# Two of layer two's three value chunks made with seven block products, beside the first eight key tiles

## The chip, the cores and the metric

The kernel runs on one core of a Trainium2 chip. The metric is device time in microseconds for one execution, from the start of the program to its end.

The engines are named as in the profile: PE is TensorE (matrix products into PSUM banks), PEld its weight loads, DVE is VectorE, ACT is ScalarE, POOL is GpSimd, and SP is the queue that starts most loads from HBM. "q" behind an engine's name means its sequencer. L629 is line 629 of the kernel before.

## The reference, cut to what matters

A two-layer decoder trunk on 256 positions of width 2048, in float32. Layer two's mixer takes one shared K and V from the normed residual stream, 12 heads of 128, and its queries from another norm of the same stream:

```
kv = _rmsnorm(x, g_kv) @ w_kv            # 2048 x 3072: K 1536 wide, V 1536 wide
k_sh, v_sh = split(kv, 2)
proj = _rmsnorm(x, nrm[0]) @ w_in_b      # q 1536 wide, qm 512 wide
o_sb = _stick_breaking(q, k_sh, v_sh)    # 12 heads, 256 queries, 256 keys
o_mem = _memory_attention(qm, mem, ...)  # 4 heads into 256 memory rows
heads = concat(o_sb, o_mem)
x = x + _rmsnorm(heads @ w_o); then the conv-gated MLP
```

V is thus 256 x 2048 times 2048 x 1536; the kernel makes it in three chunks of 512 columns.

## The kernel before, in words

**Products.** Every float32 operand is split into a rounded high part (fp32r, an ACT cast, L622) and the rest (a DVE subtraction, L623). A product takes three matmuls: high by high, low by high, high by low (`mm3`, L127). A projection whose output is wanted with positions along the free axis is made tile by tile, 128 features by 256 positions: `ws_tile` (L133) loads 1 MB of weights into one of three `raw` tiles, splits it in two halves into `whi` and `wlo` (four tiles each), and issues 16 pairs of a 512-column matmul (both parts of the input at once) and a 256-column one. `ws_pair` makes two such tiles into one `qk` tile (five of them) and multiplies by the row factors. A projection with positions along the partitions is made by chunks of 512 columns, `as_chunk` (L213): four pieces of 1 MB, 96 matmuls of 512 columns. `v_proj` (L515) is such a chunk, scaled by the row factors on the way out of PSUM.

**Seven products.** `wide` (L634) makes two chunks at once. The 256 positions are two blocks of 128, the two chunks are two blocks of columns, each pair of k tiles (a unit, eight in all) two blocks of depth; the 2 by 2 by 2 block product is done with seven products where eight is the plain count, 21 matmuls of 512 columns for a unit. It needs sums of blocks on both sides. Those of the input come from `sums_of_h` (L588): `make(i)` does five DVE operations, and a second step splits the result into `s`, here one tile of 32 KB a partition under the tag `h1`. Those of the weights are made as they come: `first_sums` (L626) loads 512 KB into a tile `d` by SP (L629) and adds another 512 KB to it by an accumulating transfer from POOL's queue (L630); `sums` (L664) takes `d` and the 768 KB of `raw` (L661) and makes a second tile `e` on DVE; `split_sums` (L680) splits `d` and `e` into the four `forms` under the tag `x`. Both `d` and `e` come from the tag `sh`, which has eleven tiles of 4 KB a partition (`bufs=11`, L66). Beside each unit runs one `ws_tile` in pieces, `ws_beside` (L152).

In `wide` nearly every instruction is pinned: it keeps the order of the program on its engine. In unit u the order is

```
PE    half of ws(u), products 1 2 3, other half of ws(u), products 7 5 6 4
SP    d(u+2), raw(u+1), weights of ws(u+1)
DVE   split d(u), split e(u), sums(u+1), split raw(u+1), add of ws(u), split weights of ws(u+1), also[u]
```

`then` is the next phase's weights, `also` a list of further steps by unit. Where an instruction is not pinned, a scheduler that plays the program through orders each engine's queue by what is ready, and a tile is handed out again when its last reader is done. `later(n, fn)` puts `fn` ahead of the n-th next piece or tile.

**Where it is used before.** In layer one for two value chunks beside eight q and k tiles (L1097), and in each MLP in five phases.

**Layer two's mixer before** (L1143 to L1163): the row factors; value chunk 0; `x_T` (L273), which transposes x on PE and writes its scaled high and low parts into `hq` (L269 on ACT, L270 on DVE); value chunks 1 and 2; four tiles of memory queries, `qm_proj`; then six times a pair of k tiles, a pair of q tiles, and `sb_pair` (L454), which puts the scores two tiles later, the transposes of the weights five and the output six tiles later. `mem_heads` (L323) puts the memory attention's steps beside the first of these tiles. At that point `sh` holds the memory keys `mk`, the memory values `mv`, the value chunks and `qm`.

Of the kernel before, what the change touches and what calls it, by code (L numbers as in the profile page):

```python
# [10 lines left out]
F32 = mybir.dt.float32  # L11
F32R = mybir.dt.float32r
BF16 = mybir.dt.bfloat16
AF = mybir.ActivationFunctionType
ALU = mybir.AluOpType
AX = mybir.AxisListType

P = 128
D = 2048
S = 256  # L20
# [4 lines left out]
KT = D // P  # L25
# [20 lines left out]
class Body:  # L46
# [538 lines left out]
        else:  # L585
            self.add_normed(ys, r[1], 1, each)

    def sums_of_h(self, h):  # L588

        nc, pin = self.nc, self.pin
        s = self.sb.tile([P, KT // 2, 4, 2, P], F32R, name="h1", tag="h1", bufs=1)

        def less(out, x, y):

            pin(nc.vector.scalar_tensor_tensor(out, x, -1.0, y, op0=ALU.mult, op1=ALU.subtract))

        def make(i):  # L600
            a, d = self.pairtile(), self.pairtile().rearrange("p a (b t) -> p (a b) t", b=2)
            hh = h[2][:, 2 * i:2 * i + 2, :, :].bitcast(F32)
            pin(nc.vector.tensor_add(a, hh[:, :, 0, :], hh[:, :, 1, :]))
            a1, a2 = a[:, :, 0:P], a[:, :, P:S]
            pin(nc.vector.tensor_sub(d[:, 0, :], a2[:, 1, :], a2[:, 0, :]))
            less(d[:, 1, :], d[:, 0, :], a1[:, 0, :])
            pin(nc.vector.tensor_sub(d[:, 2, :], a1[:, 0, :], a2[:, 0, :]))
            less(d[:, 3, :], d[:, 1, :], a1[:, 1, :])
            return lambda: self.split_heads(d, s[:, i, :, 0, :], s[:, i, :, 1, :])

        return s, make

# [21 lines left out]
    def wide(self, src, then, ahead, h, s, forms, r, beside, also, outs=None):  # L634

        nc, n = self.nc, KT // 2
        ps = {i: self.bank("g" if i in (1, 2, 6, 7) else "s") for i in range(1, 8)}
        pin, add = self.pin, nc.vector.tensor_add
        half = lambda f, i: f[..., i * 512:(i + 1) * 512]

        def lhs(i, u):
            if i in (1, 2, 4):  # L650
                kt, t = 2 * u + (i != 1), int(i == 4)
                return [h[2][:, kt, a, t * P:(t + 1) * P] for a in range(2)]
            return [s[:, u, {5: 0, 6: 1, 7: 2, 3: 3}[i], a, :] for a in range(2)]

        def product(i, u, f, at):
            self.mm3(ps[i], *lhs(i, u), half(f[0], at), half(f[1], at), u == 0, u == n - 1)

        def load(u):

            raw = self.sb.tile([P, 2048], F32, name="raw", tag="raw", bufs=3)  # L660
            pin(nc.sync.dma_start(raw[:, :1536], src[u][:, :1536]))  # L661
            return raw

        def sums(d, raw):  # L664

            e = self.sh([P, 1024])
            pin(add(half(e, 1), half(d, 0), half(raw, 2)))
            pin(add(half(e, 0), half(e, 1), half(raw, 0)))  # L668
            return d, e

        def plain(raw):
            fa, fb = ([self.sb.tile([P, 1024], F32R, name=k, tag=k, bufs=4) for k in ("whi", "wlo")]
                      for _ in range(2))
            self.split(*fa, raw[:, 0:1024])
            self.split(*(half(f, 0) for f in fb), half(raw, 2))
            return fa, fb

        summed = [[forms[:, 2 * i + j, :] for j in range(2)] for i in range(2)]

        def split_sums(t):  # L680
            for of, parts in zip(t, summed):
                self.split(*parts, of)

        raw = load(0)

        high, low = self.splits[-4]
        with self.tc.issue_after(high.ins), self.tc.issue_after(low.ins):
            t = sums(ahead.pop(0), raw)
            split_sums(t)
        b = beside[0]()  # L690
        next(b)
        next(b)
        f = plain(raw)
        self.pinned = True
        for u in range(n):
            more = u + 1 < n
            next(b)
            if u:
                split_sums(t)
            self.catch_up()  # L700
            fa, fb = f
            product(1, u, fa, 1)
            product(2, u, fa, 0)
            product(3, u, fb, 0)
            if u + 2 < n:
                ahead.append(self.first_sums(src, u + 2))
            elif then is not None:
                ahead.append(self.first_sums(then, u + 2 - n))
            if more:
                raw = load(u + 1)  # L710
                after = beside[u + 1]()
                t, f = sums(ahead.pop(0), raw), plain(raw)
            self.catch_up()
            next(b)
            next(b, None)
            if more:
                next(after)
                next(after)
            if u in also:
                also[u]()  # L720
            product(7, u, summed[0], 1)
            product(5, u, summed[0], 0)
            product(6, u, summed[1], 1)
            product(4, u, summed[1], 0)
            b = after
        g0, a, v0, v1 = outs() if outs else (self.sc([P, 512]) for _ in range(4))
        more = lambda out, x, i: pin(add(out, ps[i], x))

        def scaled(out, i, t):
            pin(nc.vector.scalar_tensor_tensor(out, ps[i], r[:, t:t + 1], out, op0=ALU.mult, op1=ALU.add))  # L730

        pin(nc.scalar.copy(a, ps[1]))
        pin(nc.scalar.activation(g0, ps[1], AF.Copy, scale=r[:, 0:1]))
        scaled(g0, 2, 0)
        more(a, a, 6)
        more(v0, a, 5)
        more(v0, v0, 3)
        more(a, a, 7)
        more(v1, a, 5)
        pin(nc.scalar.activation(a, a, AF.Copy, scale=r[:, 1:2]))  # L740
        scaled(a, 4, 1)
        self.pinned = False
        self.catch_up(-1)
        return (g0, a), (v0, v1)

    def ffn(self, layer, h, each, filler=None, done=None, late=None):
        nc = self.nc
# [240 lines left out]
    def run(self):  # L988
# [86 lines left out]
        qm = self.qm_proj(a["wqm_a"], h, 1)  # L1075

        forms = self.sb.tile([P, 4, 1024], F32R, name="x", tag="x", bufs=1)
        tiles, pairs, V = {}, {}, []

        def pair(j, out):  # L1080
            who = QK_ORDER[2 * j:2 * j + 2]
# [4 lines left out]
        def tile(u):  # L1086
            j, i = u // 2, u % 2
            if i == 0:
                pairs[j] = self.pairtile()
            done = lambda: self.behind_this(*pair(j, pairs[j]))  # L1090
            return self.ws_beside(pairs[j][:, i, :], a["wqk_a"][u], h, done if i else None)

        def outs():
            V.extend(self.sh([P, 2, 512]) for _ in range(2))
            return [v[:, t, :] for v in V for t in range(2)]

        self.wide(a["wv01_a"], None, ahead, h, s, forms, self.r, [lambda u=u: tile(u) for u in range(8)], self.rest_of(make), outs)  # L1097
        minus = self.small(2)
        nc.vector.tensor_scalar_mul(minus, self.r, -1.0)
        for t in range(2):  # L1100
            nc.scalar.activation(V[1][:, t, :], V[1][:, t, :], AF.Copy, scale=minus[:, t:t + 1])
        V.append(v2)
        self.x = sb.tile([P, 2, D], F32, name="x", tag="x", bufs=1)
        for t in range(2):
            self.later(t, lambda t=t: load(self.x[:, t, :], a["mem"][t]))
# [37 lines left out]
        with self.tc.issue_after(self.last_hi.ins):  # L1143
            self.r = self.x_rstd()
        self.later(3, spread)
        V = [self.v_proj(a["wv_b"][0], hk)]
        hq = self.hset("h1")
        self.x_T(COL_G["b0"], hq)
        V += [self.v_proj(a["wv_b"][c], hk) for c in range(1, 3)]
        qm = self.qm_proj(a["wqm_b"], hq)  # L1150
        mh, ml = self.sh([P, 4, S], F32R), self.sh([P, 4, S], F32R)
        self.mem_heads(qm, mk, mv, lambda i: (mh[:, i, :], ml[:, i, :]), 1)
        heads = {}

        def outs(hh):
            return heads[hh // 4][0][:, hh % 4, :], heads[hh // 4][1][:, hh % 4, :]

        for j in range(6):
            if j % 2 == 0 and j < 4:
                heads[j // 2] = (self.sh([P, 4, S], F32R), self.sh([P, 4, S], F32R))  # L1160
            kt = self.ws_pair(a["wk_b"][2 * j:2 * j + 2], hk, R=lambda: self.R)
            qt = self.ws_pair(a["wq_b"][2 * j:2 * j + 2], hq, R=lambda: self.Rs)
            self.sb_pair(j, qt, kt, V, outs, 0 if j == 5 else 1)  # L1163
        hh, hl, _ = self.hset("h1")
        heads[2] = (hh[:, 0:4, :], hl[:, 0:4, :])
        lhs = [(mh[:, i, :], ml[:, i, :]) for i in range(4)] + [outs(i) for i in range(12)]
# [17 lines left out]
def _feature_tiles(w):  # L1184

    n = w.shape[1] // P
    return np.ascontiguousarray(w.reshape(KT, P, n, P).transpose(2, 1, 0, 3)).reshape(n, P, KT * P)
# [37 lines left out]
def _layout(i):  # L1225
# [4 lines left out]
    for l in range(2):  # L1230
# [15 lines left out]
        "wqm_a": _feature_tiles(heads_a[:, 36:].reshape(D, 512)),  # L1246
        "wqk_a": _feature_tiles(heads_a[:, order].reshape(D, 24 * E)),
        "wo_a": _chunks(perm(i["w_o_a"][0], 512)),
        "wk_b": _feature_tiles(wkv[:, :1536]), "wv_b": _chunks(wkv[:, 1536:]),
        "wq_b": _feature_tiles(wb[:, :1536]), "wqm_b": _feature_tiles(wb[:, 1536:]),  # L1250
        "wo_b": _chunks(perm(i["w_o_b"][0], 1536)),
    }
# [22 lines left out]
```

## Time and profile before

| what | value |
|---|---|
| three runs | 2192.32, 2193.20 and 2193.99 us; median 2193.2 |
| profiled execution | 2195.61 us, of which the span is 2193.8 us |
| PE busy | 2178.6 us, 99% of the span |
| DVE busy | 1691.6 us, 77% |
| ACT busy | 1313.3 us, 60% |
| POOL busy | 161.9 us, 7% |
| moved by DMA | 525.18 MB, mean 239 GB/s |
| mean granted TensorE clock | 0.997 |

The span runs from the first to the last instruction of the program; the 1.8 us that the profiled execution has beyond it lie around the program. A row of the time line gives start, length, engine, line, operation, tiles and count, and in brackets the idle time ahead of it with what ended it. A row of the view of waits gives the sum, the number of times and the longest.

### The profile page before, as it was taken

How to read it: one execution, taken by the hardware profiler on the slowest of the kernel's cores; microseconds unless marked ns; L12 is line 12 of the kernel's file. 1: busy time of each engine (PE TensorE's matmuls, PEld its weight loads, DVE VectorE, ACT ScalarE, POOL GpSimd, SP SyncE). 2: the span in 40 equal slices, each digit the busy share in tenths (PEclk: the TensorE clock that was granted, in tenths of full speed). 3: DMA queues.
4: the chain of work that ended last, by engine and by line, in shares of the span. 5: the costliest groups of instructions: out<-in, count | busy, mean ns of one | idle time of the engine just before them, and what ended most of it. 6: DMA issues, size and time to landing. Idle time of an engine off the chain costs nothing. (4 is left out here: it accounts for less than half of the span.)

```text
span 2193.8 us, 29163 instructions
## 1 busy us (share of the span) xinstructions
PE 2178.6 (99%) x10950; PEld 1834.0 (84%) x10950; DVE 1691.6 (77%) x2260; ACT 1313.3 (60%) x1871; POOL 161.9 (7%) x183
## 2 busy tenths in 40 slices
PE   9999999999999999999999999999999999999998
PEld 7888888888888888888888888878888888888886
DVE  7798867997887868788864677569978868687786
ACT  7566746666565665656664555456665656656563
POOL 0000001010101011010000000000101010110100
PEclk9999999999999999999999999999999999999999
DMA  9886457786979879797655445567969798797974
GB/s 353 261 255 246 172 188 248 217 279 222 291 231 280 267 234 291 224 286 259 245 184 188 154 163 174 191 224 224 275 223 292 228 280 267 233 294 221 287 243 180
DMA packets 105997, 525.18 MB, mean 239 GB/s; under 512 B 10752, under 2 KB 11136, under 8 KB 66304
## 3 DMA queue, kind: packets, MB, share of 16 engines
q1 hardware_dynamic: 73728, 443.62, 56.3%
q0 software_dynamic: 32128, 79.70, 18.5%
q8 instruction: 86, 1.41, 0.2%
q14 instruction: 55, 0.45, 0.1%
HBM read 500.21 MB, written 23.07 MB: 239 GB/s over the span
## 5 line engine op out<-in xcount | busy, mean ns | idle before, releaser
L623 DVE TENSOR_TENSOR wlo<-raw,whi 128x1024 fp32r<-128x1024 f32 (+1 forms) x758 | 861.0, 1157 | 302.3 <-ACT whi L622 297.6
L622 ACT CAST whi<-raw 128x1024 fp32r<-128x1024 f32 (+1 forms) x758 | 747.3, 1000 | 417.4 <-PE ps_g L128 188.2
L163 PE MATMUL ps_s<-h,whi 128*128 128x512 f32 x1408 | 506.8, 397 | 0.0
L128 PE MATMUL ps_g<-whi,sh 128*128 128x512 f32 x1488 | 464.1, 393 | 0.0
L145 PE MATMUL ps_g<-h,whi 128*128 128x512 f32 x1080 | 388.5, 401 | 0.7 <-DVE h L270 0.7
L163 PE MATMUL ps_s<-h,wlo 128*128 128x256 f32 x1408 | 380.6, 281 | 1.1 <-DVE wlo L623 1.1
L128 PEld LDWEIGHTS ps_g<-whi,sh 128*128 128x128 f32 x1488 | 277.6, 188 | 57.6
L163 PEld LDWEIGHTS ps_s<-h,whi 128*128 128x128 f32 x1408 | 264.5, 188 | 57.1 <-ACT whi L622 0.3
L146 PE MATMUL ps_g<-h,wlo 128*128 128x256 f32 x1152 | 311.7, 281 | 0.0
L128 PE MATMUL ps_g<-wlo,sh 128*128 128x512 f32 x744 | 291.7, 392 | 0.0
L163 PEld LDWEIGHTS ps_s<-h,wlo 128*128 128x128 f32 x1408 | 265.6, 189 | 17.0 <-DVE wlo L623 1.8
L128 PE MATMUL ps_g<-whi,h 128*128 128x512 f32 x784 | 245.9, 394 | 1.3 <-ACT whi L622 1.3
L145 PEld LDWEIGHTS ps_g<-h,whi 128*128 128x128 f32 x1080 | 203.5, 188 | 47.0 <-DVE h L270 1.1
L146 PEld LDWEIGHTS ps_g<-h,wlo 128*128 128x128 f32 x1152 | 218.1, 189 | 5.6
L623 DVE TENSOR_TENSOR x<-sh,x 128x1024 fp32r<-128x1024 f32 x176 | 208.2, 1220 | 0.0
L622 ACT CAST x<-sh 128x1024 fp32r<-128x1024 f32 x176 | 176.8, 1048 | 1.6 <-DVE sh L668 1.6
L128 PEld LDWEIGHTS ps_g<-whi,h 128*128 128x128 f32 x784 | 140.4, 188 | 31.5 <-ACT whi L622 2.2
L128 PEld LDWEIGHTS ps_g<-wlo,sh 128*128 128x128 f32 x744 | 139.7, 188 | 32.2
L175 ACT COPY qk<-ps_s 128x256 f32<-128x256 f32 x88 | 32.9, 373 | 209.5 <-PE ps_s L163 209.5
L128 PE MATMUL ps_g<-wlo,h 128*128 128x512 f32 x392 | 154.0, 393 | 0.1
L128 PE MATMUL ps_g<-x,h 128*128 128x512 f32 x528 | 151.4, 394 | 0.0
L128 PE MATMUL ps_s<-x,h 128*128 128x512 f32 x528 | 151.0, 394 | 0.0
(193 smaller groups left out, 2168.9 us busy)
## 6 DMA issues: line engine op xcount, KB each, us to landing
raw<-in_up_dram SPq DMA_DIRECT2D x96, 1024.0 KB, 6.8
raw<-in_dn_dram SPq DMA_DIRECT2D x88, 1024.0 KB, 5.4
raw<-in_uw_dram SPq DMA_DIRECT2D x80, 768.0 KB, 7.6
sh<-in_uw_dram SPq DMA_DIRECT2D x80, 512.0 KB, 8.1
sh<-in_uw_dram POOLq DMA_DIRECT2D x80, 512.0 KB, 10.2
raw<-in_wqk_a_dram SPq DMA_DIRECT2D x24, 1024.0 KB, 5.0
yout<-sh POOLq DMA_DIRECT2D x32, 512.0 KB, 8.6
raw<-in_wo_b_dram SPq DMA_DIRECT2D x16, 1024.0 KB, 4.8
```

The source lines that it names most:

```text
L128: mm = lambda *o, **k: self.pin(self.nc.tensor.matmul(*o, **k))
L145: mm(b, whi[:, ks], both, start=kt == 0, stop=False)
L146: mm(b[:, 0:S], wlo[:, ks], one, start=False, stop=False)
L163: mm = lambda *o, **k: self.pin(self.nc.tensor.matmul(*o, **k))
L175: self.pin(self.nc.scalar.copy(out, b[:, S:]))
L622: high = self.pin(self.nc.scalar.copy(hi, of))
L623: low = self.pin(self.nc.vector.tensor_sub(lo, of, hi.bitcast(F32)))
```

## The change

Value chunks 0 and 1 of layer two go through `wide`, with the first eight k tiles beside the eight units. Value chunk 2 is still a plain chunk and comes first. The sums of `hk` can't lie in `h1`, which holds `hq` by then, so `sums_of_h` gets a ring: four `sh` tiles, used twice, and scratch from the tag `sc`. Units 0 to 3 are made ahead of `wide`, units 4 to 7 within it. The tag `x` is needed for `forms`, so x is stored to DRAM while the memory queries are made and loaded again some eight tiles after `wide`. The k pairs 0 to 3 wait in their `qk` tiles; k pairs 4 and 5 are made behind q pair 0 and ahead of q pair 5, so the q pairs 1 to 4 follow each other. The memory heads' steps start one tile later.

```diff
-    def sums_of_h(self, h):
+    def sums_of_h(self, h, ring=0):
...
+        if ring:
+            places = [self.sh([P, 4, 2, P], F32R) for _ in range(ring)]
+            room = lambda: self.sc([P, 2, S])
+        else:
+            whole = self.sb.tile([P, KT // 2, 4, 2, P], F32R, name="h1", tag="h1", bufs=1)
+            places = [whole[:, i] for i in range(KT // 2)]
+            room = self.pairtile
+        s = lambda u: places[u % len(places)]
...
+    def values(self, src, ahead, h, s, forms, tile, also):
...
+        self.wide(src, None, ahead, h, s, forms, self.r, [lambda u=u: tile(u) for u in range(8)], also, outs)
+        minus = self.small(2)
+        nc.vector.tensor_scalar_mul(minus, self.r, -1.0)
+        for t in range(2):
+            nc.scalar.activation(V[1][:, t, :], V[1][:, t, :], AF.Copy, scale=minus[:, t:t + 1])
+        return V
...
-        V = [self.v_proj(a["wv_b"][0], hk)]
+        v2 = self.v_proj(a["wv_b"][0], hk)
         hq = self.hset("h1")
         self.x_T(COL_G["b0"], hq)
-        V += [self.v_proj(a["wv_b"][c], hk) for c in range(1, 3)]
+
+        for t in range(2):
+            self.later(0, lambda t=t: nc.gpsimd.dma_start(self.xout[t], self.x[:, t, :]))
+        s, make = self.sums_of_h(hk, 4)
+        for i in range(4):
+            self.later(i, lambda i=i: make(i)())
+        ahead = []
+        self.later(2, lambda: ahead.extend(self.first_sums(a["wv01_b"], u) for u in range(2)))
         qm = self.qm_proj(a["wqm_b"], hq)
+        forms = self.sb.tile([P, 4, 1024], F32R, name="x", tag="x", bufs=1)
...
+        def tile(u):
+            j, i = u // 2, u % 2
+            if i == 0:
+                ks[j] = self.pairtile()
+
+            def times():
+                self.pin(nc.vector.tensor_tensor(ks[j], ks[j], self.R.unsqueeze(1).to_broadcast([P, 2, S]),
+                                                 op=ALU.mult))
+
+            return self.ws_beside(ks[j][:, i, :], a["wk_b"][u], hk, (lambda: self.behind_this(times)) if i else None)
...
+        also = {0: lambda: begin(4), 1: lambda: halves[4](), 2: lambda: begin(5), 3: lambda: halves[5](),
+                4: lambda: (begin(6), halves[6]()), 5: lambda: begin(7), 6: lambda: halves[7]()}
+        V = self.values(a["wv01_b"], ahead, hk, s, forms, tile, also) + [v2]
+        self.x = sb.tile([P, 2, D], F32, name="x", tag="x", bufs=1)
+        for t in range(2):
+            self.later(8 + t, lambda t=t: nc.gpsimd.dma_start(self.x[:, t, :], self.xout[t]))
...
-        self.mem_heads(qm, mk, mv, lambda i: (mh[:, i, :], ml[:, i, :]), 1)
+        self.mem_heads(qm, mk, mv, lambda i: (mh[:, i, :], ml[:, i, :]), 2)
...
         for j in range(6):
+            if j == 5:
+                k_pair(5)
...
-            kt = self.ws_pair(a["wk_b"][2 * j:2 * j + 2], hk, R=lambda: self.R)
             qt = self.ws_pair(a["wq_b"][2 * j:2 * j + 2], hq, R=lambda: self.Rs)
-            self.sb_pair(j, qt, kt, V, outs, 0 if j == 5 else 1)
+            self.sb_pair(j, qt, ks[j], V, outs, 0 if j == 5 else 1)
+            if j == 0:
+                k_pair(4)
```

`values` is what layer one did inline before; layer one calls it now with its own arguments. `begin(i)` is the first step of `make(i)`, `halves[i]` the second. The weights of the two chunks are laid out on the host in the four blocks that `wide` reads, as layer one's are.

More of the change, by code (lines that the diff above doesn't have):

```diff
@@ L586, in out_proj @@
             self.add_normed(ys, r[1], 1, each)
-    def sums_of_h(self, h):
+    def sums_of_h(self, h, ring=0):
         nc, pin = self.nc, self.pin
-        s = self.sb.tile([P, KT // 2, 4, 2, P], F32R, name="h1", tag="h1", bufs=1)
+        if ring:
[6 more added lines that the diff above has]
+        s = lambda u: places[u % len(places)]
         def less(out, x, y):
@@ L600, in make @@
         def make(i):
-            a, d = self.pairtile(), self.pairtile().rearrange("p a (b t) -> p (a b) t", b=2)
+            a, d = room(), room().rearrange("p a (b t) -> p (a b) t", b=2)
             hh = h[2][:, 2 * i:2 * i + 2, :, :].bitcast(F32)
@@ L608, in make @@
             less(d[:, 3, :], d[:, 1, :], a1[:, 1, :])
-            return lambda: self.split_heads(d, s[:, i, :, 0, :], s[:, i, :, 1, :])
+            return lambda: self.split_heads(d, s(i)[:, :, 0, :], s(i)[:, :, 1, :])
         return s, make
@@ L652, in lhs @@
                 return [h[2][:, kt, a, t * P:(t + 1) * P] for a in range(2)]
-            return [s[:, u, {5: 0, 6: 1, 7: 2, 3: 3}[i], a, :] for a in range(2)]
+            return [s(u)[:, {5: 0, 6: 1, 7: 2, 3: 3}[i], a, :] for a in range(2)]
         def product(i, u, f, at):
@@ L744, in wide, with outs @@
         return (g0, a), (v0, v1)
+    def values(self, src, ahead, h, s, forms, tile, also):
+        nc, V = self.nc, []
+        def outs():
+            V.extend(self.sh([P, 2, 512]) for _ in range(2))
+            return [v[:, t, :] for v in V for t in range(2)]
+        self.wide(src, None, ahead, h, s, forms, self.r, [lambda u=u: tile(u) for u in range(8)], also, outs)
[4 more added lines that the diff above has]
+        return V
     def ffn(self, layer, h, each, filler=None, done=None, late=None):
@@ L1077, in run @@
         forms = self.sb.tile([P, 4, 1024], F32R, name="x", tag="x", bufs=1)
-        tiles, pairs, V = {}, {}, []
+        tiles, pairs = {}, {}
         def pair(j, out):
@@ L1091, in tile @@
             return self.ws_beside(pairs[j][:, i, :], a["wqk_a"][u], h, done if i else None)
[L1093 to L1102, printed above, removed]
+        V = self.values(a["wv01_a"], ahead, h, s, forms, tile, self.rest_of(make)) + [v2]
         self.x = sb.tile([P, 2, D], F32, name="x", tag="x", bufs=1)
@@ L1145, in run, with begin @@
         self.later(3, spread)
-        V = [self.v_proj(a["wv_b"][0], hk)]
+        v2 = self.v_proj(a["wv_b"][0], hk)
         hq = self.hset("h1")
         self.x_T(COL_G["b0"], hq)
-        V += [self.v_proj(a["wv_b"][c], hk) for c in range(1, 3)]
-        qm = self.qm_proj(a["wqm_b"], hq)
+        for t in range(2):
[5 more added lines that the diff above has]
+        self.later(2, lambda: ahead.extend(self.first_sums(a["wv01_b"], u) for u in range(2)))
+        qm = self.qm_proj(a["wqm_b"], hq)
+        forms = self.sb.tile([P, 4, 1024], F32R, name="x", tag="x", bufs=1)
+        ks, halves = {}, {}
+        def tile(u):
[6 more added lines that the diff above has]
+            return self.ws_beside(ks[j][:, i, :], a["wk_b"][u], hk, (lambda: self.behind_this(times)) if i else None)
+        def begin(i):
+            halves[i] = make(i)
+        also = {0: lambda: begin(4), 1: lambda: halves[4](), 2: lambda: begin(5), 3: lambda: halves[5](),
[4 more added lines that the diff above has]
+            self.later(8 + t, lambda t=t: nc.gpsimd.dma_start(self.x[:, t, :], self.xout[t]))
         mh, ml = self.sh([P, 4, S], F32R), self.sh([P, 4, S], F32R)
-        self.mem_heads(qm, mk, mv, lambda i: (mh[:, i, :], ml[:, i, :]), 1)
+        self.mem_heads(qm, mk, mv, lambda i: (mh[:, i, :], ml[:, i, :]), 2)
         heads = {}
@@ L1156, in outs, with k_pair @@
             return heads[hh // 4][0][:, hh % 4, :], heads[hh // 4][1][:, hh % 4, :]
+        def k_pair(j):
+            ks[j] = self.ws_pair(a["wk_b"][2 * j:2 * j + 2], hk, R=lambda: self.R)
         for j in range(6):
+            if j == 5:
+                k_pair(5)
             if j % 2 == 0 and j < 4:
                 heads[j // 2] = (self.sh([P, 4, S], F32R), self.sh([P, 4, S], F32R))
-            kt = self.ws_pair(a["wk_b"][2 * j:2 * j + 2], hk, R=lambda: self.R)
             qt = self.ws_pair(a["wq_b"][2 * j:2 * j + 2], hq, R=lambda: self.Rs)
-            self.sb_pair(j, qt, kt, V, outs, 0 if j == 5 else 1)
+            self.sb_pair(j, qt, ks[j], V, outs, 0 if j == 5 else 1)
+            if j == 0:
+                k_pair(4)
         hh, hl, _ = self.hset("h1")
@@ L1248, in _layout @@
         "wo_a": _chunks(perm(i["w_o_a"][0], 512)),
-        "wk_b": _feature_tiles(wkv[:, :1536]), "wv_b": _chunks(wkv[:, 1536:]),
+        "wk_b": _feature_tiles(wkv[:, :1536]), "wv_b": _chunks(wkv[:, 2560:]),
+        "wv01_b": _units(wkv[:, 1536:2560], (0,))[0],
         "wq_b": _feature_tiles(wb[:, :1536]), "wqm_b": _feature_tiles(wb[:, 1536:]),
```

## The prediction

> **What bounds the kernel now.** I read the page first, then PE's waits, then the time line of layer one's value stage, which is the change's own code at work, then SP's waits and the loads' times.
>
> ```profile
> span 2193.8 us, 29163 instructions
> PE 2178.6 (99%) x10950; PEld 1834.0 (84%) x10950; DVE 1691.6 (77%) x2260; ACT 1313.3 (60%) x1871; POOL 161.9 (7%) x183
> ...
> PE ps_s L280 <- DVE x L541: 2.1, 1, 2.1
> ...
> PE ps_s L163 <- DVE wlo L623: 1.1, 2, 0.6
> PE ps_g L145 <- DVE h L270: 0.7, 1, 0.7
> ```
>
> PE is never idle for more than about 2 us in one place, and only 15 us in all. So whatever takes matmuls away shortens the run by their issue time, as long as everything else keeps PE fed; and any new wait of PE is added whole, since no slack absorbs it. The sum is made against the profiled execution's 2195.6 us (span 2193.8) and carried over as a difference to the median 2193.2, which is 0.1% lower.
>
> **What is removed on PE.** Price of a plain chunk: between the first evacuations of chunks 1 and 2. Price of a plain tile: between two evacuations of `qm`. Price of a unit of `wide`: from one unit's first matmul to the next one's, in layer one (unit 3 to unit 4; its last four products begin at 137.36).
>
> ```profile
> 1159.75 0.69 ACT L524 ACTIVATE sh<-ps_g,small 128x512 f32<-128x512 f32 x1 [1.89 <-PE ps_g L128]
> ...
> 1181.51 0.69 ACT L524 ACTIVATE sh<-ps_g,small 128x512 f32<-128x512 f32 x1 [1.89 <-PE ps_g L128]
> ...
> 1189.78 0.37 ACT L149 COPY sh<-ps_g 128x256 f32<-128x256 f32 x1 [1.84 <-PE ps_g L148]
> 1195.42 0.37 ACT L149 COPY sh<-ps_g 128x256 f32<-128x256 f32 x1 [1.89 <-PE ps_g L148]
> ...
> 129.62 0.40 PE L163 MATMUL ps_s<-h,whi 128*128 128x512 f32 x1
> ...
> 137.36 0.86 PE L128 MATMUL ps_g<-x,h 128*128 128x512 f32 x3
> ...
> 140.14 0.40 PE L163 MATMUL ps_s<-h,whi 128*128 128x512 f32 x1
> ```
>
> A chunk is 21.76 us (96 matmuls, 0.227 each), a tile 5.64, a unit 10.52. Before: two chunks and eight k tiles, 43.5 + 45.1 = 88.6 us. After: eight units, 84.2 us. Gain **4.5 us**, if layer two's units run at layer one's pace.
>
> **What lets layer one keep that pace: the loads are early.** These are DVE's and SP's rows around the same unit.
>
> ```profile
> 132.33 2.36 DVE L623 TENSOR_TENSOR x<-sh,x 128x1024 fp32r<-128x1024 f32 x2
> ...
> 135.20 0.69 DVE L667 TENSOR_TENSOR sh<-sh,raw 128x512 f32<-128x512 f32 x1
> ...
> 136.53 1.82 DVE L623 TENSOR_TENSOR wlo<-raw,whi 128x1024 fp32r<-128x1024 f32 x2
> 138.27 0.42 DVE L176 TENSOR_TENSOR qk<-ps_s,qk 128x256 f32<-128x256 f32 x1
> 138.92 2.36 DVE L623 TENSOR_TENSOR wlo<-raw,whi 128x1024 fp32r<-128x1024 f32 x2 [0.22 <-ACT whi L622]
> ...
> 141.80 2.35 DVE L623 TENSOR_TENSOR x<-sh,x 128x1024 fp32r<-128x1024 f32 x2
> ...
> 117.13 0.47 SPq L629 DMA_DIRECT2D sh<-in_wv_a_dram  x1
> 120.27 0.33 SPq L661 DMA_DIRECT2D raw<-in_wv_a_dram  x1
> ...
> 126.58 0.50 SPq L629 DMA_DIRECT2D sh<-in_wv_a_dram  x1
> ```
>
> In unit 3 SP issues d(5) and then raw(4). They went out at 117.13 and 120.27, 12.5 and 9.4 us before the unit began on PE (129.62). sums(4) runs at 135.20, so raw(4) had 14.9 us to land. And DVE has nothing to spare from there: after the sums come the split of raw, the add, and the first half of ws(4)'s weights, done at about 140.1, when PE begins unit 4 (140.14).
>
> **What changes: the tiles that d and e live in.** Layer one's stage held five `sh` tiles (`mk`, `mv`, the third value chunk, `qm`, the rope tables) and had six for d and e. Layer two after the change holds `mk`, `mv`, `v2`, `qm` and the ring's four places, eight of eleven; all are read until `wide` ends or later. That leaves **three**. When unit u begins, these are d(u), e(u) and d(u+1). So d(u+2) can be issued only when DVE has split d(u), inside unit u, and everything behind it on SP waits too: raw(u+1), and ws(u+1)'s weights. That SP does stand at this line for want of an `sh` tile is seen before, at the MLP phases' borders:
>
> ```profile
> SPq L629 <- DMA yout<-sh: 25.9, 4, 7.9
> ...
> SPq L629 <- PE ps_g L128: 24.1, 8, 3.0
> ```
>
> Up to 7.9 us at once, with no PE wait from it: the lead above is larger. Here the delay is more than the lead.
>
> **Its price.** The split of d is the first half of the rows at 132.33 and 141.80: it ends about 3.9 us after unit 3's start and 2.8 after unit 4's (units with and without the sums of h before it), mean 3.4. Then 0.5 for SP to issue d(u+2); then raw(u+1) must land:
>
> ```profile
> raw<-in_wv_a_dram SPq DMA_DIRECT2D x8, 768.0 KB, 6.2
> sh<-in_wv_a_dram SPq DMA_DIRECT2D x8, 512.0 KB, 8.0
> sh<-in_wv_a_dram POOLq DMA_DIRECT2D x8, 512.0 KB, 8.3
> ...
> xout<-x POOLq DMA_DIRECT2D x4, 1024.0 KB, 8.1
> ...
> DMA to landing us min/median/max: 4.1/6.5/7.4
> ```
>
> The last row is line 661 in layer one's stage alone. I take 6.2, the median of the eight: raw now goes out right between d's 512 KB and the 1 MB of ws(u+1), so neither alone (4.1) nor behind more than the loads it met before. From the sums to the next unit's first matmul is 140.14 - 135.20 = 4.9. So a unit that waits like this lasts 3.4 + 0.5 + 6.2 + 4.9 = 15.0 us, 4.5 more than 10.5. Which units: d(2) takes d(0)'s tile, which is split long before `wide` begins, so unit 0 is free. d(3) to d(7), issued in units 1 to 5, each wait. Units 6 and 7 have no d to fetch. **Five times 4.5: 22.5 us.** With the shortest landing, 4.1, it is 12.9 a unit and 12 us; with the longest, 7.4, 16.2 and 28.5 us. d itself is late as well, but has a whole unit more: issued 3.4 into unit u, landed 8.0 later, plus 8.3 for POOL's accumulation, about 20 after the start; the sums that read it come at 15.0 + 10.1 = 25.
>
> **x outside.** Two 1 MB stores and two 1 MB loads on POOL's queue. `forms` can't be written before the stores have landed, but they go out at the first of four `qm` tiles, some 20 us ahead; the loads come at tiles 8 and 9 of about 16 before x is used again. Cost nothing; POOL's queue is 7% busy and only d's accumulations stand behind the stores. If the cover went, 8.1 us once.
>
> **x_T directly ahead of its reader.** Before, 43.5 us of value chunks lay between `x_T` and the first `qm` tile; now none.
>
> ```profile
> L269 ACT ACTIVATE h<-ps_s,cols 128x256 fp32r<-128x256 f32 x16 | 6.4, 487 | 0.6 <-PE ps_s L280 0.6
> L270 DVE SCALAR_TENSOR_TENSOR h<-ps_s,cols,h 128x256 fp32r<-128x256 f32 x16 | 6.8, 479 | 0.1
> ```
>
> Sixteen k tiles at 0.48 us on either engine are 7 to 8 us, beside a first `qm` tile that eats them in 5.6. The same neighbours at layer two's MLP cost PE the 0.7 us in the waits above. DVE also has the first sums, splits and the tile splits in that stretch. I take **2 us**, near the 0.7; ends 0 and 4.5. The four `make`s ahead of `wide` read only `hk` and can fall into chunk 2's time, where DVE is half idle (third busy time: 2.45 of 5 us):
>
> ```profile
> 1126.00:1131.00 5.00, 5.00 (x25) 4.17 (x24) 2.45 (x2) 1.67 (x3) 0.10 (x1) 1.00 0.53 170
> ```
>
> **q pairs behind each other.** One round of two k, two q tiles and one `sb_pair`:
>
> ```profile
> 1265.04:1290.82 25.78, 25.78 (x152) 22.62 (x151) 18.28 (x26) 13.22 (x19) 0.00 (x0) 1.00 0.47 164
> ...
> L188 DVE TENSOR_TENSOR qk<-qk,Rs 128x512 f32<-128x512 f32 x6 | 4.1, 684 | 0.0
> ```
>
> The columns are length, then busy time of PE, PEld, DVE, ACT and POOL. Taking two tiles out (PE 11.3; DVE four splits of 1.2, two adds of 0.4 and a 0.7 multiplication, 6.3) leaves DVE 12.0 in 14.5 us of PE. It fits; k pair 4 and q pairs wait for scores to free a `qk` tile, but PE has four banks ahead. Zero; ends 0 and 2.
>
> Sum: -4.5 + 22.5 + 2 = **+20 us**: 2193.2 + 20 = **2213 us** (0.9% slower), own range 2200 to 2224.
>
> **The clock.** When PE stood 2.1 us and then had only transposes and short bursts, its clock was halved:
>
> ```profile
> 1458.00:1462.00 4.00, 1.90 (x17) 1.55 (x15) 2.77 (x6) 1.31 (x4) 2.43 (x5) 1.00 0.90 154
> 1462.00:1466.00 4.00, 3.28 (x15) 2.73 (x13) 3.47 (x9) 2.49 (x7) 0.58 (x1) 0.51 1.02 311
> 1466.00:1470.00 4.00, 4.00 (x20) 3.67 (x19) 2.63 (x6) 2.24 (x6) 0.00 (x0) 0.64 0.95 318
> 1470.00:1474.00 4.00, 4.00 (x24) 3.48 (x23) 2.85 (x5) 3.84 (x9) 0.00 (x0) 1.00 0.01 4
> ```
>
> The third column from the right is the clock: 0.51, 0.64, 1.00, some 3.4 us of work lost for one gap. The change makes five gaps of 4.5 us. A unit with 3.4 us lost needs 13.9 us of PE, still under the 15.0 it waits for, so I count it as hidden. The Trainium skill ("TensorE: Matmul & The Clock Gate", section on HAM oscillation) has it that an idle window of about 3.4 us halves the clock, so that every one of these gaps would do it; the rows above agree on the halving, after a shorter gap. By it the sum is the rival that follows, if the loss isn't hidden.
>
> **The rivals.** *The clock adds up.* Each late unit also runs part of its work at half clock, the add of ws(u) and the splits behind it on ACT come late, and the loss stands beside the wait: 5 x 3.4 = 17 more, 2230. For it: five gaps longer than the one above. Against it: the 1.1 us between 13.9 and 15.0. Chance 0.12.
>
> *The wait never bites* (not slower). If one of the eight tiles that I count as held is free in `wide`, d(u+2) takes the tile that was split a unit earlier. raw(4) then goes out 10.5 us sooner than by my account, at about 123.5 where I have 134.0, lands at 129.7 and is there before 135.20; units stay at 10.5. That point decides: three tiles, or four. Then 2193.2 - 4.5 + 0.7 to 2: 2189 to 2191. For it: layer one's six tiles show no wait at all. Against it: each of the eight has a reader after `wide` or in its last units. Chance 0.15, of it 0.08 beyond 0.2%.
>
> *Something small elsewhere turns it further* (the q stretch, the start of `wide`): above 2232 without the clock, 0.03. My forecast has 0.70.
>
> The range leaves out the second rival and a little above: 2197 to 2232. Faster 0.08, within 0.2% 0.08, slower 0.84; 0.2% is about what a measurement can tell here.
>
> **What the profile after would show.** SP waiting at line 629 for DVE's split of `x`, some 10 us each, five times; the 768 KB load right behind; DVE idle ahead of the sums (L667's successor) with that load as releaser; PE waits of 3 to 6 us on `wlo` or `whi` at the k tiles' first matmuls in units 2 to 6; units of about 15 us, and 10.5 for units 0 and 7; 24 fewer 512-column matmuls. Wrong would be: units of 10.5 throughout, or a clock that stays halved.

## The result and the profile after

| | before | after |
|---|---|---|
| median | 2193.16 us, 6 runs (2192.32 to 2193.99) | 2208.18 us, 6 runs (2206.75 to 2209.33) |
| profiled execution, span | 2195.6, 2193.8 us | 2207.9, 2206.1 us |

The changed kernel takes 1.0068 times as long, 95% interval 1.0058 to 1.0078: 15.0 us slower. In the kernel after, the split into high and low parts is L629 (ACT) and L630 (DVE), `first_sums` L636 (SP) and L637 (POOL), the 768 KB load L668, the sums L674.

From the page of the kernel after, the busy line and the chain that ended last:

```profile
span 2206.1 us, 29290 instructions
PE 2178.5 (99%) x10926; PEld 1830.9 (83%) x10926; DVE 1734.2 (79%) x2348; ACT 1327.1 (60%) x1896; POOL 173.7 (8%) x195
...
PE 94%; DVE 2%; DMA 1%; issue 1%; ACT 0%; SPq 0%; POOL 0%; POOLq 0%; DVEq 0%; ACTq 0%
```

PE has its 24 matmuls fewer and is just as long busy as before (2178.6), because some of them ran at half clock, as the table of units shows. Waits of PE, SP and DVE in the kernel after (sum, times, longest):

```profile
PE ps_s L163 <- DVE qk L176: 8.9, 4, 4.0
PE ps_s L163 <- DVE wlo L630: 3.8, 7, 0.6
...
PE ps_g L145 <- DVE h L270: 1.0, 1, 1.0
PE ps_s L280 <- DVE h L270: 0.3, 1, 0.3
...
SPq L636 <- DVE x L630: 60.6, 5, 15.4
SPq L636 <- PE ps_g L128: 31.6, 9, 7.5
...
DVE sh L674 <- DMA raw<-in_wv_b_dram: 20.7, 4, 5.8
```

Read from the bottom: DVE stands four times before the sums for the 768 KB load, SP stands before the load of `d` that goes ahead of it until DVE has split an older `d` into `x` (the forms), and PE stands at the first matmul of a k tile. Of SP's five waits for `x`, one (6.1 us, for d(2)) lies ahead of the stage; the four in the stage make 54.5. The new stage by units, each from its first L163 matmul to the next unit's (length; busy PE, PEld, DVE, ACT, POOL; clock; DMA share; GB/s):

```profile
1164.54:1175.05 10.51, 10.51 (x55) 8.84 (x53) 6.50 (x10) 5.15 (x8) 0.37 (x1) 1.00 0.54 140
1175.05:1188.36 13.31, 10.67 (x54) 8.69 (x53) 8.59 (x14) 4.67 (x7) 1.20 (x1) 1.00 0.65 208
1188.36:1202.83 14.47, 12.51 (x54) 10.04 (x54) 9.26 (x12) 6.26 (x9) 1.20 (x1) 0.88 0.71 203
1202.83:1218.38 15.55, 10.96 (x53) 8.74 (x54) 9.62 (x15) 5.82 (x8) 1.20 (x1) 0.95 0.62 192
1218.38:1232.72 14.34, 13.16 (x54) 10.43 (x54) 9.20 (x12) 6.16 (x9) 1.20 (x1) 0.82 0.66 199
1232.72:1244.17 11.45, 10.84 (x54) 8.84 (x54) 10.40 (x16) 7.31 (x10) 1.20 (x1) 1.00 1.02 320
1244.17:1255.44 11.27, 10.71 (x55) 8.82 (x54) 11.11 (x17) 5.85 (x8) 0.00 (x0) 1.00 0.58 202
1255.44:1265.95 10.51, 10.51 (x55) 8.84 (x53) 9.72 (x11) 7.53 (x10) 0.00 (x0) 1.00 0.76 280
sum 101.41, PE 89.87 PEld 73.23 DVE 74.40 ACT 48.74 POOL 6.36; mean PE 11.23 PEld 9.15 DVE 9.30 ACT 6.09 POOL 0.79
```

101.4 us stand where the two chunks and eight tiles before took 88.6: 12.8 more. With `x_T`'s 1.3 that is 14.1. The gap of PE at the layer's MLP (L280 for x) ended at 1460.79 before and at 1475.57 after, 14.8 later; the remaining 0.7 I can't put to a row. Units 1 to 4 are the long ones. SP's rows show what starts them:

```profile
1179.00 0.33 SPq L636 DMA_DIRECT2D sh<-in_wv_b_dram  x1
1179.38 0.42 SPq L668 DMA_DIRECT2D raw<-in_wv_b_dram  x1
...
1192.30 0.33 SPq L636 DMA_DIRECT2D sh<-in_wv_b_dram  x1
1192.67 0.44 SPq L668 DMA_DIRECT2D raw<-in_wv_b_dram  x1
...
1207.81 0.33 SPq L636 DMA_DIRECT2D sh<-in_wv_b_dram  x1
1208.19 0.43 SPq L668 DMA_DIRECT2D raw<-in_wv_b_dram  x1
...
1222.27 0.33 SPq L636 DMA_DIRECT2D sh<-in_wv_b_dram  x1
1222.64 0.43 SPq L668 DMA_DIRECT2D raw<-in_wv_b_dram  x1
...
1231.15 0.33 SPq L636 DMA_DIRECT2D sh<-in_wv_b_dram  x1
```

and the chain of work cut to unit 2 and its end shows the rest of the way (start, length, what):

```profile
1191.06 1.23 DVE x L630
1192.28 0.02 issue
1192.30 0.33 SPq L636
1192.63 0.04 issue
1192.67 6.39 DMA raw<-in_wv_b_dram
...
1199.19 0.70 DVE sh L674
...
1200.53 1.05 DVE wlo L630
1201.58 0.08 issue
1201.66 0.68 DVE wlo L630
1202.34 0.34 DVE qk L176
```

No PE row stands in this chain: the split of `d`, the next `d`'s issue, the load behind it, the sums, the split of raw, the add of the k tile, and then PE begins unit 3 at 1202.83.

### The profile page after: what moved, and what is told of

Read it like the earlier page. It is cut to its first block, busy times and chain, and to the rows that moved or that the text cites. A ratio compares the mean times of both kernels' runs of the same rounds, so it can differ in the third digit from the quotient of the medians.

```text
span 2206.1 us, 29290 instructions
## 1 busy us (share of the span) xinstructions
PE 2178.5 (99%) x10926; PEld 1830.9 (83%) x10926; DVE 1734.2 (79%) x2348; ACT 1327.1 (60%) x1896; POOL 173.7 (8%) x195
## 4 chain that ended last, share of the span: by engine, by line
PE 94%; DVE 2%; DMA 1%; issue 1%; ACT 0%; SPq 0%; POOL 0%; POOLq 0%; DVEq 0%; ACTq 0%
PE ps_g L128 39%; PE ps_s L163 24%; PE ps_s L128 11%; PE ps_g L145 10%; PE ps_g L146 5%; DVE wlo L630 1%; DMA raw<-in_wv_b_dram 1%; PE ps_s L922 1%; PE ps_g L148 1%; PE ps_s L280 1%; DMA raw<-in_wmv_dram 0%; PE ps_s L335 0%; PE ps_s L362 0%; DMA sh<-in_uw_dram 0%; DVE x L630 0%
## 5 line engine op out<-in xcount | busy, mean ns | idle before, releaser
L630 DVE TENSOR_TENSOR wlo<-raw,whi 128x1024 fp32r<-128x1024 f32 (+1 forms) x758 | 854.3, 1150 | 257.8 <-ACT whi L629 249.5
L629 ACT CAST whi<-raw 128x1024 fp32r<-128x1024 f32 (+1 forms) x758 | 741.5, 993 | 433.0 <-PE ps_g L128 174.9
L163 PE MATMUL ps_s<-h,whi 128*128 128x512 f32 x1536 | 555.9, 398 | 8.9 <-DVE qk L176 8.9
L163 PE MATMUL ps_s<-h,wlo 128*128 128x256 f32 x1536 | 416.9, 282 | 3.8 <-DVE wlo L630 3.8
L163 PEld LDWEIGHTS ps_s<-h,whi 128*128 128x128 f32 x1536 | 290.3, 189 | 73.0 <-ACT whi L629 11.0
L145 PE MATMUL ps_g<-h,whi 128*128 128x512 f32 x960 | 345.5, 401 | 1.1 <-DVE h L270 1.0
L163 PEld LDWEIGHTS ps_s<-h,wlo 128*128 128x128 f32 x1536 | 291.3, 190 | 22.1 <-DVE wlo L630 6.2
L146 PE MATMUL ps_g<-h,wlo 128*128 128x256 f32 x1024 | 277.4, 281 | 0.0
L630 DVE TENSOR_TENSOR x<-sh,x 128x1024 fp32r<-128x1024 f32 x192 | 226.9, 1217 | 0.3 <-ACT x L629 0.3
L128 PE MATMUL ps_g<-whi,h 128*128 128x512 f32 x688 | 215.4, 394 | 1.5 <-ACT whi L629 1.5
L145 PEld LDWEIGHTS ps_g<-h,whi 128*128 128x128 f32 x960 | 180.5, 188 | 42.4 <-DVE h L270 1.8
L146 PEld LDWEIGHTS ps_g<-h,wlo 128*128 128x128 f32 x1024 | 193.6, 189 | 4.9
L629 ACT CAST x<-sh 128x1024 fp32r<-128x1024 f32 x192 | 192.6, 1045 | 1.5 <-DVE sh L675 1.5
L637 POOL DMA_DIRECT2D sh<-in_uw_dram x80 | 98.6, 1232 | 662.6 <-DMA sh<-in_uw_dram 335.5
## 6 DMA issues: line engine op xcount, KB each, us to landing
sh<-in_uw_dram POOLq DMA_DIRECT2D x80, 512.0 KB, 10.5
```

The lines of the kernel that those rows point to most:

```text
L128: mm = lambda *o, **k: self.pin(self.nc.tensor.matmul(*o, **k))
L145: mm(b, whi[:, ks], both, start=kt == 0, stop=False)
L146: mm(b[:, 0:S], wlo[:, ks], one, start=False, stop=False)
L163: mm = lambda *o, **k: self.pin(self.nc.tensor.matmul(*o, **k))
L629: high = self.pin(self.nc.scalar.copy(hi, of))
L630: low = self.pin(self.nc.vector.tensor_sub(lo, of, hi.bitcast(F32)))
```

## The experiments

The theory is the prediction's: three free `sh` tiles make SP stand, and the 768 KB load behind it is late. Its rivals are that VectorE is too full, that x's transfers or the accumulations disturb the loads, and that the halved clock makes the time. "Units" below are lengths from first matmul to first matmul, as in the table. Each ratio is against the kernel before on the same chip, with its 95% interval. The kernel before took 2193.5 to 2194.2 us beside these runs and 2193.2 beside the change, so a difference between a run and the change is good to about 1 us.

**Four tiles in place of three.** One of the ring's places gets the room of the mask, which nothing reads any more by then (its last read in this run is at 303 us).

```diff
-            places = [self.sh([P, 4, 2, P], F32R) for _ in range(ring)]
+            places = [self.sh([P, 4, 2, P], F32R) for _ in range(ring - 1)]
+            places.append(self.sb.tile([P, 4, 2, P], F32R, name="mask", tag="mask", bufs=1))
...
-        self.mask = sb.tile([P, 3, S], F32, name="mask")
+        self.mask = sb.tile([P, 3, S], F32, name="mask", tag="mask", bufs=1)
```

> The changed kernel with one of the ring's four places moved to the tag of the layer-one mask, so that four sh tiles instead of three are left for d and e; nothing else differs. Theory (SP stands at d's load for want of a tile, with raw and the k tile's weights behind it): with four tiles d(u+2) can go out a unit earlier, units of layer two's stage fall from 13 to 15.5 us to 10.5 to 11, SP no longer waits for the split of x; time 2193.2 - 4.5 + 1.3 = 2190 us (2187 to 2194). Rival, VectorE is the bound in that stage (a fourth set of sums of h and the multiplication of k within it): nothing changes, 2208 us, units stay at 13 to 15.5. Rival, the gaps come from the clock or from the traffic of x to DRAM: 2205 to 2208.

Measured 2192.10 us, ratio 0.9994 (0.9985 to 1.0004): 16 us less than the change. The units are 10.45 to 10.51 us, but for unit 6 with 11.28. SP's wait and what is left of PE's in this kernel (its lines are one higher):

```profile
SPq L637 <- DVE x L631: 28.7, 4, 9.3
...
PE ps_s L163 <- DVE wlo L631: 1.7, 3, 0.6
```

SP still stands four times for a tile, for 7 us on average, and PE loses nothing by it: the load is a unit ahead. VectorE's work, x's transfers and the accumulations are those of the change, so these three rivals fall as causes of the 15 us. The halved clock can't be judged from this run, since the gaps that halve it are gone too; it is taken up below.

**The same step in layer one, with nothing of the change.** In the kernel before, tiles are held through layer one's value stage by a tiny first write ahead of it and a tiny read behind it; layer one has six free, so three held leave three and two held leave four.

```diff
+        held = [self.sh([P, 1024]) for _ in range(3)]      # or 2
+        for t in held:
+            self.tc.keep_in_program_order(nc.vector.memset(t[:, 0:2], 0.0))
         v2 = self.v_proj(a["wv_a"][0], h)
...
         self.wide(a["wv01_a"], None, ahead, h, s, forms, self.r, ...)
+        for t in held:
+            self.tc.keep_in_program_order(nc.vector.tensor_scalar_mul(self.small(2), t[:, 0:2], 1.0))
```

Three held:

> The kernel before, again with three sh tiles held in layer one, now from ahead of the third value chunk until the last evacuation of the stage (in the earlier try they were free again 2 us after being written, at 101.9 us, so only units 0 and 1 met three tiles). Theory: units 1 to 5 wait, as no ring place comes free here: 12.3 to 15.5 us each, 2193.5 + 5 x 4 = 2213 us (2208 to 2218). If the stall needs anything else of the change (the fourth set of sums inside, x's traffic, the q order): 2193.5 to 2198 us.

Measured 2218.37 us, ratio 1.0112 (1.0096 to 1.0128), 24 us more and 0.4 above the range; units 10.52, 14.37, 17.42, 14.61, 15.77, 14.53, 11.6. Unit 2 is the longest: its sums (136.36) ran 8.1 us behind the issue of their load (128.25), more than the longest landing that the prediction took. Two held:

> The kernel before with two sh tiles held through the whole of layer one's value stage by a first and a last tiny operation in program order: four tiles are left for d and e. With three held in the same way the stage gave units of 14.4 to 17.4 and 2218. Theory, that the step is between three and four free tiles: no late unit, the stage's units stay at 10.5 and the time at 2193 to 2195. Rival, that each tile fewer makes the loads later by a part: units of some 12 us and 2203 to 2208.

Measured 2193.47 us, ratio 1.0000 (0.9991 to 1.0009); all units 10.46 to 10.52. SP's waits, first with three held, then with two:

```profile
SPq L629 <- DVE x L623: 73.0, 5, 16.9
```

```profile
SPq L629 <- DVE x L623: 28.6, 4, 9.2
```

So the loss needs neither layer two's k tiles, nor x outside, nor the ring: it is the number of tiles, with the step between four (nothing) and three (24 us).

Two earlier forms of this, with the hold begun later and the reads behind `minus`, missed as tests, because the scheduler put the reads inside the stage (with three held, the tiles were written at 99.98 and read at 101.78).

```diff
         qm = self.qm_proj(a["wqm_a"], h, 1)
+        held = [self.sh([P, 1024]) for _ in range(3)]      # or 2, and the writes as above
...
         V.append(v2)
+        for t in held:
+            self.tc.keep_in_program_order(nc.vector.tensor_scalar_mul(self.small(2), t[:, 0:2], 1.0))
```

> The kernel before, with three sh tiles held over layer one's stage of seven products (written by a tiny memset ahead of it, read by a tiny multiplication behind it), so that three are left there too instead of six. No work of the change is in it. Theory: the same stall appears in layer one, units 1 to 5 last 13 to 15.5 us instead of 10.5, SP waits for the split of x some 10 to 15 us each time; 2193.2 + 5 x 4 = 2213 us (2206 to 2218). Rival VectorE, and every rival that needs the rest of the change (x outside, order of the q pairs): 2193 us.

Measured 2197.96 us, ratio 1.0018 (1.0007 to 1.0028): only units 0 and 1 were late (12.31 and 13.16).

> The kernel before with two sh tiles held over layer one's stage, so that four are left. Theory: d(u+2) takes a tile that was split a unit earlier, the loads lose some lead and still land ahead of the sums: units of 10.5, 2193 us (2192 to 2196). If each tile taken away costs something by itself: a third to two thirds of what the run with three held costs, 2198 to 2206 us.

Measured 2193.62 us, ratio 1.0000 (0.9990 to 1.0009). The tiles were held as briefly here, so it says little by itself.

**The fifth wait.** In the change d(7) went out at 1231.15, 1.6 us before unit 5 began, though d(5) was not split yet. The tile that it took should be the ring's place 0, whose last reader is unit 4's products. In the changed kernel, place 0 is read once more behind the stage:

```diff
         self.wide(src, None, ahead, h, s, forms, self.r, ...)
+        if also.get(6):
+            self.tc.keep_in_program_order(
+                nc.vector.tensor_scalar_mul(self.small(2), s(0)[:, 0, 0, 0:2].bitcast(F32), 1.0))
```

> The changed kernel with ring place 0 read once more, by a tiny multiplication behind the stage's last evacuation. Theory: in the changed kernel d(7) went out 1.6 us ahead of unit 5 because place 0, last read by unit 4's products, had come free; held, d(7) waits for the split of d(5) like the four before it, unit 5 lasts 13.5 to 15.5 us instead of 11.5: 2208.2 + 3 = 2211 us (2210 to 2213). If unit 5 was short for another reason: 2208 us.

Measured 2217.05 us, ratio 1.0105 (1.0091 to 1.0119): 8.9 more than the change (7.9 if each is set against its own kernel before), where 3 were expected. d(7) now waits until 1240.69, and the units are 10.5, 14.18, 14.67, 15.55, 14.47, 16.58, 13.91: unit 5 is the fifth late one, 5.1 longer than in the change, unit 1 0.9 and unit 6 2.6 longer. SP's waits, then units 5 to 7 (the windows begin 0.07 us early):

```profile
SPq L636 <- DVE x L630: 77.1, 6, 15.9
...
SPq L636 <- PE ps_g L128: 24.1, 8, 3.0
...
1233.90:1250.48 16.58, 11.00 (x53) 8.77 (x53) 10.34 (x15) 6.18 (x9) 1.20 (x1) 0.99 0.56 183
1250.48:1264.39 13.91, 13.37 (x53) 10.97 (x54) 11.46 (x17) 7.06 (x10) 0.00 (x0) 0.77 0.80 274
1264.39:1274.90 10.51, 10.51 (x55) 8.84 (x54) 9.73 (x12) 7.60 (x10) 0.00 (x0) 1.00 0.58 201
```

The step (who frees the tile) is shown: the ninth wait for `ps_g`, 7.5 us in the change, is gone, and a sixth wait for `x` is there in its place. The size was off twice. In unit 5 `d` goes out 6.7 us after the start, not about 4, since a whole set of the sums of h (set 6, made and split) runs on DVE ahead of the split of d(5). And unit 6 follows a gap of 4.96 us at a clock of 0.77 and has no wait of its own: PE is busy for 13.37 of its 13.91 us.

**The load of d behind the others.** With three tiles, SP issues raw(u+1) and ws(u+1)'s weights first and d(u+2) last.

```diff
-            if u + 2 < n:
+            if u + 2 < n and not last:
                 ahead.append(self.first_sums(src, u + 2))
...
+            if last and u + 2 < n:
+                ahead.append(self.first_sums(src, u + 2))
```

> The changed kernel, but in layer two's stage SP gets d(u+2) behind raw(u+1) and the weights of the k tile u+1, not ahead of them; still three tiles for d and e. Theory: what hurts is what stands behind d on SP, not d itself. raw(u+1) is then on time; d(u+2) goes out some 3 to 4 us into unit u, lands with its accumulation about 11 to 13 us later, 15 to 17 us after the unit's start, where its sums want it at about 15 to 16: units of 10.5 to 12, time 2190 to 2198 us. Rival, it is d's own lateness (load and accumulation in a row): units stay at 13 and above, 2204 to 2210 us. Rival VectorE: 2208 us.

Measured 2201.47 us, ratio 1.0033 (1.0022 to 1.0045), between both accounts: units 10.45, 10.51, 10.47, 11.48, 11.42, 12.78, 14.41. Freeing the loads that stood behind SP's wait gives back 6.7 us. What is left is another loss: `d` still goes out 4 to 7 us into its unit, and in shorter units the sums come sooner and stand for its accumulation by POOL, which in the change they never did. So the run shows that the loads behind the wait matter, but it doesn't split the change's 15 us. POOL's issue of the last accumulation, and DVE's sums behind it:

```profile
1230.64 1.20 POOL L637 DMA_DIRECT2D sh<-in_wv_b_dram  x1 [11.09 <-DMA sh<-in_wv_b_dram]
...
1242.85 0.69 DVE L674 TENSOR_TENSOR sh<-sh,raw 128x512 f32<-128x512 f32 x1 [4.12 <-DMA sh<-in_wv_b_dram]
```

**x_T earlier.** With four tiles, `x_T` goes ahead of the plain value chunk, as cover for its 1.3 us; then also the sums of h for units 6 and 7 are spread (the edit is below).

```diff
-        v2 = self.v_proj(a["wv_b"][0], hk)
         hq = self.hset("h1")
         self.x_T(COL_G["b0"], hq)
+        v2 = self.v_proj(a["wv_b"][0], hk)
```

> The run with four tiles, and x_T ahead of the third value chunk, so that its 32 transposes and their evacuations do not stand directly ahead of the memory queries that read them. Theory: the 1.0 and 0.3 us of PE waiting for h there go, 2192.1 - 1.3 = 2190.8 us. If the waits only move to the value chunk: 2192.

Measured 2194.3 us, ratio 1.0001 (0.9992 to 1.0010). The waits on `h` are gone, but unit 0 takes 13.08, since the first sums are late on VectorE, behind an accumulation:

```profile
1160.58 0.69 DVE L675 TENSOR_TENSOR sh<-sh,raw 128x512 f32<-128x512 f32 x1 [5.88 <-DMA sh<-in_wv_b_dram]
```

> The run before, and the last two sets of sums of h spread: begin(6) in unit 4, its split in unit 5, unit 7's set whole in unit 6. Theory: in the run with four tiles only unit 6 was late (11.3 us, PE waiting 0.5 us for wlo), as VectorE has 2.4 us of sums between units 4 and 5 and 1.7 after unit 5; spread, unit 6 falls to 10.5: 2190.8 - 0.8 = 2190 us. If unit 6 is late because raw(7) is: 2191.

Measured 2193.39 us, ratio 0.9997 (0.9988 to 1.0006). Unit 6 falls from 11.20 to 10.54 as expected, unit 0 rises to 13.89. So what `x_T` costs has moved into unit 0 and grown, not gone.

**Four tiles and the sums spread.** Only the two edits that paid are kept: the first one, and

```diff
-                4: lambda: (begin(6), halves[6]()), 5: lambda: begin(7), 6: lambda: halves[7]()}
+                4: lambda: begin(6), 5: lambda: halves[6](), 6: lambda: (begin(7), halves[7]())}
```

> The change with four free sh tiles (one ring place in the mask's tag), x_T where the change has it, and the sums of h for units 4 to 7 spread so that unit 4 only begins place 6, unit 5 ends it, and unit 6 begins and ends place 7. Four tiles without the spreading gave units of 10.45 to 10.51 but one of 11.28 (unit 6) behind sums bunched on VectorE. Theory: unit 6 falls to 10.5, all else stays; 0.8 us off the run with four tiles, 2191.3 (2189.5 to 2193), about 0.1% under the kernel before and at the limit of what can be told. Rival, that the extra unit length is not VectorE's order but a late load: unit 6 stays at 11.3 and the time at 2192.1.

Measured 2190.91 us, ratio 0.9988 (0.9979 to 0.9997): 2.6 us under the kernel before, a difference that the interval only just sets apart from none, and 17 under the change. Unit 6 falls to 10.47, as expected. The first and the last unit and the sum of the eight in its windows:

```profile
1164.52:1175.03 10.51, 10.51 (x55) 8.84 (x53) 6.50 (x10) 5.15 (x8) 1.20 (x1) 1.00 0.86 288
...
1237.97:1248.44 10.47, 10.47 (x55) 8.84 (x54) 9.46 (x14) 7.64 (x10) 0.00 (x0) 1.00 0.48 163
sum 83.92, PE 83.92 PEld 70.69 DVE 72.89 ACT 49.09 POOL 5.99; mean PE 10.49 PEld 8.84 DVE 9.11 ACT 6.14 POOL 0.75
```

PE is never idle in the stage. 83.9 in place of 88.6 is 4.7 us, the prediction's first term of 4.5; less 1.3 for `x_T`, 3.4 should be left, and the gap at the MLP does end 2.9 us earlier than before (1457.90 against 1460.79).

## Why the prediction was right, and what was mis-sized

**The gain** of 4.5 us is there (84.2 forecast, 83.9 measured with four tiles), and the loss outweighs it, as forecast.

**Three tiles, and SP stands**: right, and shown from both sides: by one tile more in the change, and by three fewer in layer one. The rival that the wait never bites needed a fourth tile; that is just the point on which the prediction said it would turn.

**A late unit's price**, 15.0: measured from the rows of SP and DVE, in units 1 to 4:

| step | forecast | unit 1 | 2 | 3 | 4 | mean |
|---|---|---|---|---|---|---|
| unit's start to d's issue | 3.4 | 3.95 | 3.94 | 4.98 | 3.89 | 4.2 |
| to raw's issue | 0.5 | 0.38 | 0.37 | 0.38 | 0.37 | 0.4 |
| to the sums | 6.2 | 5.34 | 6.52 | 6.56 | 6.44 | 6.2 |
| to the next unit's start | 4.9 | 3.64 | 3.64 | 3.63 | 3.64 | 3.6 |
| sum | 15.0 | 13.31 | 14.47 | 15.55 | 14.34 | 14.4 |

The last term was read from a unit that wasn't late: there PE itself set the next start, so 4.9 was only an upper bound. In a late unit PE starts when DVE has done the sums, the split of raw and the add of the k tile, whose one bank PE needs; the first low half of the weights comes 0.6 later. So the first releaser in PE's waits is `qk` at L176, not `wlo` or `whi` as forecast, and its four waits in the stage are 2.6, 1.3, 4.0 and 0.9 us, not 3 to 6. The first term was too short for units 2 to 4: behind a late unit PE begins right after the add, with nearly all of the weights' split (2.4 us) still ahead of `d`'s on DVE, where in layer one 1.2 us of it had run by then.

**Five such units**: this step failed. The tiles were counted as held until `wide` ends or later, but the ring's place 0 is free after unit 4's products. SP's wait for `ps_g` shows it: 24.1 in 8 before, 31.6 in 9 after, and 24.1 in 8 again with place 0 held. Four units were late, by 2.8, 4.0, 5.0 and 3.8, and units 5 and 6 by 0.9 and 0.8, together 17.3 where 22.5 were forecast. Of the 5.2 between them the fifth unit is 3.6 (0.9 in place of 4.5) and the price of the four 2.4 (15.6 in place of 18.0), less 0.8 for unit 6, which was not forecast. Without these 5.2 the forecast of 2213 comes to 2208. That it then meets the measurement so closely is partly luck: `x_T` was forecast 0.7 too high, and 0.7 measured has no row.

**The clock**: PE idled 11.5 us in the stage (101.4 less 89.9 busy), which is less than the 17.3; the rest is that PE's own work took longer, 5 us of it by half clock (the units' 0.88, 0.95 and 0.82). It was counted as hidden in the wait, and in the kernel after it was: the chain through unit 2 has no PE in it, although that unit ran at 0.88, and from the sums to the next unit's start it is 3.64 us in unit 4 at 0.82 as in unit 1 at 1.00. It was close, though: the profile's chain through unit 4 does run over PE. With place 0 held the half clock was not hidden: the unit behind the last gap has no wait to hide it in and took 13.91 us, 3.4 more than 10.5. So the rival had its mechanism right but not its size: once for the last gap, not five times.

**x_T** cost 1.3 (forecast 2), in the two waits on `h`. **x outside** and **the q pairs** show no PE wait; what they may have cost lies in the 0.7 that no row carries. The loads of `d` themselves had lead enough, as forecast; with SP's order turned round they had not.

## What to carry to other kernels

Before a stage is copied to another place, count the free tiles of each tag that its loads take, unit by unit with each tile's last reader; a queue that stands for a tile also holds back what is issued behind it, and that, not the waiting load, was first to be late here. A wait of the queue is harmless while its loads are a unit ahead: the same line waited 28.7 us at no cost and 60.6 us at 17. Read the terms of a path that is to become critical from a place where they set the end; where another engine sets it, they are bounds.

## What was not expected of the hardware

PE's clock changes in pieces of 3.41 us, and the length of a gap alone doesn't decide. In each trace here every recorded change lies a whole multiple of 3.413 us behind the first (in the kernel after: 1189.47, 1192.89, 1216.78, 1223.61, 1476.19, 1479.61). So time falls into windows that run on whatever PE does. Here they are around the gap of 2.03 us at the MLP, first in the kernel after, then in the one with four tiles and spread sums (the prediction shows the kernel before, at 0.51):

```profile
1472.78:1476.19 3.41, 1.38 (x12) 1.05 (x10) 2.19 (x5) 0.73 (x3) 2.58 (x6) 1.00 0.74 118
1476.19:1479.60 3.41, 3.29 (x14) 2.67 (x13) 3.41 (x8) 2.97 (x7) 0.58 (x1) 0.50 1.02 357
```

```profile
1453.22:1456.63 3.41, 2.66 (x14) 1.96 (x12) 1.51 (x4) 0.69 (x2) 1.97 (x3) 1.00 0.30 64
1456.63:1460.04 3.41, 1.54 (x12) 1.29 (x12) 3.33 (x6) 1.20 (x3) 1.77 (x4) 1.00 1.12 276
1460.04:1463.46 3.42, 2.87 (x19) 2.48 (x20) 3.28 (x9) 2.86 (x8) 0.58 (x1) 1.00 0.99 261
```

The same gap of 2.03 us cost a window of half clock in the one and nothing in the other. In the first the whole gap lies in one window (busy 1.38, idle 2.03). In the second it is spread over two, and the fuller one has 1.87 idle. Cut into such windows, the twelve traces here agree: a window at full clock in which PE idled 2.03 us or more was followed by half clock every time, one with 1.78 or less never, and from 1.82 to 1.88 there are both. A window at half clock was followed by full clock where PE idled 0.24 us or less in it, and by a second at half clock from 0.36 on. That is why such a stretch was 3.41 or 6.83 us long, but for the last one, which the program's end cuts; in the stage after, the gaps of 2.64 and 3.98 us had one, those of 1.33 and 0.90 had none.

The Trainium skill ("TensorE: Matmul & The Clock Gate", Part 1) says that a free-running window of about 3.4 us is watched and that an idle one halves the clock. The windows of 3.413 us agree; but here 2.03 us of idle time within one window was enough.
